# Chain transfers through DRAM issued from GpSimd's queue instead of SyncE's, in a two-layer hybrid trunk

## Chip, cores and metric

The kernel runs on one core of one Trainium2 chip. The metric is the device time of one execution, in microseconds; the time of a version is the median of its runs.

## What is computed

The reference is a causal trunk of two layers over 1024 tokens of 1024 channels, in float32. Each layer is a norm, a wide input projection, two token mixers side by side, an output projection and a gated MLP with a causal convolution of width 3. Layer 0 mixes with GLA (4 heads) and S5 (16 groups of 16 channels); layer 1 with RWKV-7 (8 heads of 64) and Mamba-2 (8 heads in 2 groups).

```python
for i in range(DEPTH):                       # two layers
    h = rms_norm(x, norm_mix[i])
    if i % 2 == 0:
        p = h @ e_w_in[j]
        ya = gla_mixer(p[..., :GLA_COLS], ...)
        yb = s5_mixer(p[..., GLA_COLS:], ...)
        x = x + jnp.concatenate([ya, yb], axis=-1) @ e_w_out[j]
    else:
        p = h @ o_w_in[j]
        yc = rwkv7_mixer(p[..., :RWKV_COLS], ...)
        yd = mamba2_mixer(p[..., RWKV_COLS:], ...)
        x = x + jnp.concatenate([yc, yd], axis=-1) @ o_w_out[j]
    h = rms_norm(x, norm_ffn[i])
    x = x + conv_glu_ffn(h, ffn_w_up[i], ..., ffn_w_down[i])
return rms_norm(x, norm_final)
```

Three places of the mixers matter here. GLA takes `b = jnp.cumsum(gc, axis=2)`, the running sum of its log decays. S5 gives `y = Re(C s) + d * u` and then `gelu(y)` and a gate. RWKV-7 divides keys by their length and its outputs by their standard deviation, head by head, and Mamba-2 normalizes its output group by group: a reciprocal root of one number for each token and head (or group).

## The kernel before

The 1024 tokens are done in two halves of 512 (`h` is 0 or 1). The projections are the bulk: each weight is split into a high and a low part and each product is three matmuls of 128x512 (`mm3`). `wunit` brings one unit of weights: SyncE loads 256 KB into `wr`, ScalarE rounds it to `wh`, VectorE takes the remainder `wl`. There are three buffers each of `wr`, `wh` and `wl`, so SyncE's next load waits until VectorE has read the buffer.

The mixers are generators that run beside the projections. `tick` advances them by the time that the projection's matmuls are thought to give; the scheduler that builds the program then places every instruction by a simulated time and a priority, so that the order on each engine is fixed when the program is built. On the chip each engine, and each engine's DMA issuing, goes through its own list in order: an instruction that waits holds back everything that stands behind it there. Buffers of the mixers come from small arenas (`k2`, `k4`, `kf`, and `mx` in PSUM).

In before nearly every DMA is issued by SyncE: weights, the projections' outputs to DRAM and back, and the mixers' own detours through DRAM. `self.MQ` and `self.Q` are both SyncE's queue; `self.AQ` is ScalarE's, which issues 14 small stores. The detours that the change touches:

- `rsqrt_rows` (14 times, in layer 1 alone: per half once for the keys, once for each of four RWKV pairs, once for each of two Mamba groups): one row per head lies in PSUM; ScalarE copies it to SBUF and issues a store (L463); a load brings it back spread over 128 partitions (`sm`, L467); VectorE does some 12 small operations; a store (L469) puts the roots into DRAM.
- `rows_to` (36 transfers): loads a row of roots broadcast over 64 or 128 partitions (L476). For the keys it fills `kk` in `rwkv_prep`; for outputs it fills `sq`, and VectorE multiplies by it next.
- GLA: `gla_decays` stores the four heads' running sums (L662), `gla_head` loads its own (L681), 8 of each.
- S5: the output `ys` (512 KB) goes to DRAM (L1045) and comes back in 8 loads of 32 KB for each of two tiles (`yf`, L1053), 32 loads in all. After each tile's eight loads VectorE forms `y`, ScalarE squares it, and so on to the gate.

GpSimd has little to do in before: it zeroes buffers (`tp` of S5 at L965, `Zs` of each RWKV pair at L1327) and clears a small tile `idle` 14 times for each `lagging` (L226); the latter only push the scheduler's placement of matmuls, and no matmul waits for them on the chip.

The tiles in the sections below: `acc` is a projection's PSUM, `kf` its copy in SBUF, `mh` and `ml` the split outputs of the mixers that the output projection reads, `yl` their load from DRAM, `dr` a buffer in DRAM, `k` any arena buffer.

Of the kernel before, what the change touches and what calls it, by code (L numbers as in the profile page):

```python
# [23 lines left out]
T = L // NH  # L24
# [104 lines left out]
class Kernel:  # L129
    def __init__(self, ctx, tc, a, dump=None):  # L130
        self.tc, self.nc, self.a = tc, tc.nc, a
        self.dump = dump
        nc = tc.nc
        self.V, self.A, self.G, self.PE, self.Q = nc.vector, nc.scalar, nc.gpsimd, nc.tensor, nc.sync
        self.MQ = nc.sync

        self.AQ = nc.scalar
        pool = lambda name, **kw: ctx.enter_context(tc.tile_pool(name=name, **kw))
        self.cp = pool("const", bufs=1)
        wp, mp = pool("stream", bufs=1), pool("mix", bufs=1)  # L140
        pp = pool("psum", bufs=1, space=PSUM)
        self.dp = pool("scratch", bufs=1, space=DRAM)
        self.uid = 0
        self.steps, self.ticks = None, 0
        self.rbc, self.rtok = [None] * NH, [None] * NH
        self.cost, self.ready, self.side = 0.0, set(), None
        self.wr = Ring(wp, "wr", WB[0], 512)
        self.wh = Ring(wp, "wh", WB[1], 512, F32R)
        self.wl = Ring(wp, "wl", WB[2], 512, F32R)
        self.xh = Ring(wp, "xh", KT, T, F32R)  # L150
        self.xl = Ring(wp, "xl", KT, T, F32R)
        self.mh = Ring(wp, "mh", MR, T, F32R)
        self.ml = Ring(wp, "ml", MR, T, F32R)
        self.yr = Ring(wp, "yr", YB[0], T)
        self.yl = Ring(wp, "yl", YB[1], T)
        self.rb = Ring(mp, "rb", 2, T)
        self.smr = Ring(mp, "sm", 24, 32)
        self.lsr = Ring(mp, "ls", 8, 32)
        self.smf = Ring(mp, "smf", 8, 8)
        self.zfr = Ring(mp, "zf", 2, 2 * RN)  # L160
        self.r0r = Ring(mp, "r0", 2, 2 * RN)
        self.gsr = Ring(mp, "gs", 2, GV)
        self.lsf = Ring(mp, "lsf", 2, 8)
        self.junk = mp.tile([128, GV], F32, name="junk")
        self.accr = Ring(pp, "acc", 4, 512)
        self.k2a, self.k4a, self.kfa = Arena(mp, "k2", K2, 520), Arena(mp, "k4", K4, 1024), Arena(mp, "kf", KF, 514)
        self.mxa = Arena(pp, "mx", 4, 512)
        self.wsa = Arena(mp, "ws", 2, 512)
# [288 lines left out]
    def rsqrt_rows(self, src, scale, bias, op1):  # L457

        p, n = src.shape[0], src.shape[0] * T // 128
        row = self.k2([p, T])  # L460
        self.act(row, src)
        d = self.dram([2, p, T])
        self.AQ.dma_start(d[0], row)  # L463
        self.fr(row)
        spread = lambda i: d[i].rearrange("a (q n) -> (a q) n", n=n)
        x = self.sm(n)
        self.MQ.dma_start(x, spread(0))  # L467
        self.ts(x, x, scale, bias, MUL, op1)
        self.MQ.dma_start(spread(1), self.rsqrt(x, n))  # L469
        return d[1]  # L470

    def rows_to(self, t, rows):

        w = 128 // rows.shape[0]
        for i in range(rows.shape[0]):
            self.MQ.dma_start(t[w * i:w * i + w], rows[i:i + 1].to_broadcast([w, T]))  # L476


    def norm_stats(self, h, t0=0, n=T, get=None, far=False):
# [158 lines left out]
    def gla_decays(self, h, wa2, alo):  # L638
# [17 lines left out]
        for hd in range(GH):  # L656
            n, b = N[hd // 2][:, hd % 2], self.k2()
            self.stt(n, E[hd // 2][:, hd % 2], -1.0, n, MUL, ADD)
            for c in range(NT):
                s = slice(c * 128, c * 128 + 128)  # L660
                self.V.tensor_tensor_scan(b[:, s], self.ones, n[:, s], 0.0, op0=MUL, op1=ADD)
            self.MQ.dma_start(self.st_b[h][hd], b)  # L662
            self.fr(b)
            yield
        self.fr(*E, *N)
# [3 lines left out]
    def gla_head(self, h, hd):  # L669
        yield from self.need(("gla", h, hd))  # L670
        qk, v, g, sg = self.k4([128, 2, T]), self.k4([128, NT, GV]), self.k4([128, NT, GV]), self.k4([128, NT, GV])
# [6 lines left out]
        self.fr(g)  # L678
        yield
        b = self.k2()  # L680
        self.MQ.dma_start(b, self.st_b[h][hd])  # L681
        c4 = lambda t: t.rearrange("p (c t) -> p c t", c=NT)
        cs = lambda c: slice(c * 128, c * 128 + 128)
        att = self.k2()
# [292 lines left out]
    def s5(self, h):  # L977
# [7 lines left out]
        for half in range(2):  # L985
            for ri in range(2):
                m = self.loaded(self.Ind[ri, half], [128, 512])
                for gg in range(8):
                    g = half * 8 + gg
# [7 lines left out]
        t = self.k2([128, 8, SN])  # L997
# [3 lines left out]
        for ri in range(2):  # L1001
# [7 lines left out]
            w = self.k2([128, 8, SN + 1])  # L1009
# [8 lines left out]
        t = self.k2([128, 8, SN + 1])  # L1018
# [6 lines left out]
        yd = self.dp.tile([SJ, SC, SG, SN], F32, tag="s5yd", bufs=2, name=self.nm("s5yd"))  # L1025
        ys = self.k4([128, SG, SN])
        ps = [self.mx([128, 8, SN]) for _ in range(2)]
        for half in range(2):
            ca = [self.loaded(self.CAd[ri, half], [128, 4, 128]) for ri in range(2)]
            tp = [self.loaded(self.Tpd[half, :, q * 4:q * 4 + 4], [128, 4, 128]) for q in range(2)]  # L1030
            for gg in range(8):
                g = half * 8 + gg
# [9 lines left out]
            self.act(ys.rearrange("p (a b) n -> p a b n", b=2)[:, :, i], ps[i])  # L1042
        self.fr(*ps)
        yield
        self.Q.dma_start(yd.rearrange("j c g n -> (j c) g n"), ys)  # L1045
        self.fr(ys, U, *X)
        yield
        z = []
        for tl in range(2):
            u = self.loaded(self.st_u[h][tl], [128, SJ, SN])  # L1050
            yf = self.k2([128, SJ, SN])
            for g in range(8):
                self.Q.dma_start(yf[16 * g:16 * g + 16], yd[:, :, tl * 8 + g, :].rearrange("j c n -> c j n"))  # L1053
            y = self.k2()
            yv = y.rearrange("p (c j) -> p j c", j=SJ)
            self.stt(yv, u, self.col("s5d", tl), yf, MUL, ADD)
# [847 lines left out]
```

## Time and profile before

| | |
|---|---|
| median of 3 runs | 2765.3 us (2763.23 to 2768.43) |
| the profiled execution | 2759.85 us |
| its span, first to last instruction | 2758.1 us |
| TensorE busy | 2663.3 us (97%) |
| VectorE busy | 1902.5 us (69%) |
| ScalarE busy | 1133.8 us (41%) |
| GpSimd busy | 79.1 us (3%) |
| mean granted TensorE clock | 0.980 |

A matmul's time is modelled and overlaps the next one's, so that 97% means that TensorE seldom lacked work, not that it worked at its peak; idle time in front of a matmul is what a wait costs. Waits are attributed to the instruction or DMA whose semaphore came last. DMA queue q1 is SyncE's and q10 ScalarE's; there is none of GpSimd's in the trace of before.

### The profile page before, as it was taken

Reading aid. Unit: us, or ns where it says so; the run is one execution under the profiler, and the core shown is the slowest. Engines: PE = TensorE matmul, PEld = TensorE weight load, DVE = VectorE, ACT = ScalarE, POOL = GpSimd, SP = SyncE. Lnnn points to the kernel's source line nnn. Section 1 sums busy time; section 2 is a strip of 40 time slices with the busy share of each in tenths; the row PEclk is TensorE's granted clock in tenths of the full one; section 3 lists DMA queues with packets and bytes.
Section 4 is the critical chain, followed back from the end, with each engine's and each line's share of the span. In section 5 each row is a group of like instructions: output and inputs, shape, how many; then the busy total and the mean of one; then the engine's idle time right before and its main releaser. Section 6 shows DMA issues by size and latency. Waiting matters only on the chain.

```text
span 2758.1 us, 39904 instructions
## 1 busy us (share of the span) xinstructions
PE 2663.3 (97%) x13804; PEld 2134.5 (77%) x13804; DVE 1902.5 (69%) x4538; ACT 1133.8 (41%) x2035; POOL 79.1 (3%) x462
## 2 busy tenths in 40 slices
PE   8999899999999999999999999999999998999998
PEld 6878788888888867777787777777687776788886
DVE  6987268766356665868586876768676687867557
ACT  4554255443234433433344544343333354434333
POOL 0000000000000000000220000000004000000000
PEclk9999799999899999999999999999999999999999
DMA  7555464434234554433343556443333345434333
GB/s 220 173 162 168 125 185 112 112 108 141 78 109 119 157 164 130 110 85 110 82 117 92 135 158 183 127 123 100 91 96 88 89 134 134 127 96 127 96 97 87
DMA packets 279602, 340.83 MB, mean 124 GB/s; under 512 B 101988, under 2 KB 137508, under 8 KB 279400
## 3 DMA queue, kind: packets, MB, share of 16 engines
q1 hardware_dynamic: 279168, 338.12, 43.2%
q8 instruction: 108, 1.77, 0.3%
q14 instruction: 94, 0.77, 0.1%
q10 hardware_dynamic: 232, 0.17, 0.0%
HBM read 286.91 MB, written 49.63 MB: 122 GB/s over the span
## 4 chain that ended last, share of the span: by engine, by line
PE 58%; DVE 7%; DMA 4%; issue 2%; ACT 1%; SPq 0%; POOL 0%; DVEq 0%; ACTq 0%
PE acc L340 49%; PE mx L340 8%; DMA k<-dr 3%; DVE k L215 2%; DVE k L245 1%; DVE wl L215 1%; DVE kf L245 1%; DMA yl<-dr 1%; ACT k L210 1%; ACT wh L210 0%; PE mx L347 0%; DVE x L215 0%; DMA dr<-kf 0%; DVE ml L215 0%; DMA rb<-dr 0%
## 5 line engine op out<-in xcount | busy, mean ns | idle before, releaser
L210 ACT ACTIVATE wh<-wr 128x512 fp32r<-128x512 f32 (+1 forms) x802 | 496.3, 620 | 933.0 <-PE acc L340 798.8
L215 DVE TENSOR_TENSOR wl<-wr,wh 128x512 fp32r<-128x512 f32 (+1 forms) x800 | 541.3, 678 | 417.9 <-ACT wh L210 378.9
L340 PE MATMUL acc<-xh,wh 128*128 128x512 f32 x2000 | 795.7, 399 | 16.8 <-ACT xh L210 9.6
L340 PE MATMUL acc<-xl,wh 128*128 128x512 f32 x2000 | 791.1, 396 | 0.1
L340 PE MATMUL acc<-xh,wl 128*128 128x512 f32 x1984 | 783.6, 396 | 7.1 <-DVE wl L215 7.0
L340 PEld LDWEIGHTS acc<-xh,wh 128*128 128x128 f32 x2000 | 377.3, 189 | 111.7 <-ACT xh L210 14.7
L340 PEld LDWEIGHTS acc<-xh,wl 128*128 128x128 f32 x1984 | 375.6, 189 | 89.6 <-DVE wl L215 10.0
L340 PEld LDWEIGHTS acc<-xl,wh 128*128 128x128 f32 x2000 | 377.1, 189 | 82.7 <-issue 3.8
L340 PE MATMUL acc<-mh,wh 128*128 128x512 f32 (+1 forms) x972 | 386.4, 399 | 25.4 <-DVE x L215 13.7
L340 PE MATMUL acc<-ml,wh 128*128 128x512 f32 (+1 forms) x972 | 385.5, 397 | 0.0
L340 PE MATMUL acc<-mh,wl 128*128 128x512 f32 (+1 forms) x972 | 383.3, 395 | 0.3 <-DVE wl L215 0.3
L215 DVE TENSOR_TENSOR k<-k,k 128x64 f32<-128x64 f32 (+27 forms) x894 | 284.6, 331 | 38.2 <-ACT k L210 19.2
L340 PEld LDWEIGHTS mx<-k,k 128*64 128x64 f32 (+5 forms) x2572 | 215.2, 154 | 82.1 <-issue 20.2
L340 PE MATMUL mx<-k,k 128*64 128x64 f32 (+9 forms) x2572 | 261.2, 256 | 11.0 <-DVE yr L215 3.5
L340 PEld LDWEIGHTS acc<-mh,wh 128*128 128x128 f32 x972 | 184.8, 190 | 68.4 <-issue 8.1
L340 PEld LDWEIGHTS acc<-mh,wl 128*128 128x128 f32 x972 | 184.1, 190 | 37.1 <-issue 2.1
L340 PEld LDWEIGHTS acc<-ml,wh 128*128 128x128 f32 x972 | 184.6, 190 | 34.0 <-issue 1.0
L210 ACT ACTIVATE k<-mx 128x512 f32<-128x512 f32 (+5 forms) x160 | 80.4, 512 | 176.6 <-PE mx L340 142.2
L210 ACT ACTIVATE k<-k 128x512 f32<-128x512 f32 (+4 forms) x176 | 109.0, 627 | 90.7 <-DVE k L215 46.2
L215 DVE TENSOR_TENSOR x<-acc,x 128x512 f32<-128x512 f32 (+1 forms) x196 | 123.2, 671 | 28.5 <-PE acc L340 28.1
L215 DVE TENSOR_TENSOR k<-k 128x256 f32<-128x256 f32 (+4 forms) x267 | 88.4, 357 | 26.0 <-DMA k<-dr 22.9
L245 DVE SCALAR_TENSOR_TENSOR kf<-acc,cols,kf 128x511 f32<-128x511 f32 (+1 forms) x132 | 98.3, 745 | 3.4 <-ACT kf L210 2.5
(178 smaller groups left out, 2360.8 us busy)
## 6 DMA issues: line engine op xcount, KB each, us to landing
wr<-wup SPq DMA_DIRECT2D x352, 256.0 KB
wr<-wdn SPq DMA_DIRECT2D x176, 256.0 KB
wr<-w1fm SPq DMA_DIRECT2D x104, 256.0 KB
dr<-kf SPq DMA_DIRECT2D x72, 256.0 KB
k<-dr SPq DMA_DIRECT2D x72, 256.0 KB
yl<-dr SPq DMA_DIRECT2D x64, 256.0 KB
wr<-wout SPq DMA_DIRECT2D x64, 256.0 KB
wr<-w0fm SPq DMA_DIRECT2D x40, 256.0 KB
```

Of the source, the lines that this page charges most:

```text
L210: self.made = self.A.activation(out, in_, f, **kw)
L215: self.made = self.V.tensor_tensor(out, a, b, op=op)
L245: self.made = self.V.scalar_tensor_tensor(out, a, s, b, op0=op0, op1=op1)
L340: return self.PE.matmul(out, lhsT, rhs, start=start, stop=stop)
```

## The change

A second name, `GQ`, is given to GpSimd's queue, and eight `dma_start` calls are moved to it: in a run 14 + 14 + 36 transfers of the roots, 8 + 8 of GLA's decays and 2 + 32 of S5's outputs, 114 in all. What they move, their buffers and the waits on their data stay. Line numbers grow by two.

```diff
         self.MQ = nc.sync
+
+        self.GQ = nc.gpsimd
 ...
-        self.MQ.dma_start(x, spread(0))
+        self.GQ.dma_start(x, spread(0))
         self.ts(x, x, scale, bias, MUL, op1)
-        self.MQ.dma_start(spread(1), self.rsqrt(x, n))
+        self.GQ.dma_start(spread(1), self.rsqrt(x, n))
 ...
         for i in range(rows.shape[0]):
-            self.MQ.dma_start(t[w * i:w * i + w], rows[i:i + 1].to_broadcast([w, T]))
+            self.GQ.dma_start(t[w * i:w * i + w], rows[i:i + 1].to_broadcast([w, T]))
 ...
-            self.MQ.dma_start(self.st_b[h][hd], b)
+            self.GQ.dma_start(self.st_b[h][hd], b)
 ...
-        self.MQ.dma_start(b, self.st_b[h][hd])
+        self.GQ.dma_start(b, self.st_b[h][hd])
 ...
-        self.Q.dma_start(yd.rearrange("j c g n -> (j c) g n"), ys)
+        self.GQ.dma_start(yd.rearrange("j c g n -> (j c) g n"), ys)
 ...
-                self.Q.dma_start(yf[16 * g:16 * g + 16], yd[:, :, tl * 8 + g, :].rearrange("j c n -> c j n"))
+                self.GQ.dma_start(yf[16 * g:16 * g + 16], yd[:, :, tl * 8 + g, :].rearrange("j c n -> c j n"))
```

Since the scheduler simulates the queues, the order on other engines moves too. Three places are shown.

SyncE's list in the first half of layer 0, where S5's outputs come back (`k20_165` is the second tile's `yf`, `wout0` the output projection's weights); before:

```order
L1053 DMA k20_165<-s5yd_111_2697 16x8x64
L417 DMA wr1_70<-wout0 128x512
L1053 DMA k20_165<-s5yd_111_2697 16x8x64 x2
L417 DMA wr2_71<-wout0 128x512
L1053 DMA k20_165<-s5yd_111_2697 16x8x64
L417 DMA wr0_69<-wout0 128x512
L1053 DMA k20_165<-s5yd_111_2697 16x8x64 x3
```

In the change the same loads stand on GpSimd's list, between GLA's decays of the two halves (`k26_171` is the first tile's `yf`):

```order
L683 DMA k29_174<-dr_58_283 128x512
L1047 DMA s5yd_111_2697<-k47_183 128x1024
L1055 DMA k26_171<-s5yd_111_2697 16x8x64 x8
L1055 DMA k20_165<-s5yd_111_2697 16x8x64 x8
L664 DMA dr_59_284<-k22_167 128x512
```

The store and the sixteen loads now follow each other with no load of weights between.

ScalarE's list at the same place. `k28_173` is the second tile's `y`, `k24_169` its square; `kf1` to `kf3` empty the PSUM banks `acc1` to `acc3`, which the output projection's first matmuls write next. Before:

```order
L210 ACTIVATE wh0_72<-wr0_69 128x512
L210 ACTIVATE k24_169<-k28_173 128x512
L210 ACTIVATE kf1_186<-acc1_162 128x384
L210 ACTIVATE kf2_187<-acc2_163 128x384
L210 ACTIVATE kf3_188<-acc3_164 128x384
L210 ACTIVATE k24_169<-k24_169 128x512
L210 ACTIVATE kf0_185<-acc0_161 128x512
```

In the change:

```order
L212 ACTIVATE kf1_186<-acc1_162 128x384
L212 ACTIVATE kf2_187<-acc2_163 128x384
L212 ACTIVATE wh1_73<-wr1_70 128x512
L212 ACTIVATE kf3_188<-acc3_164 128x384
L212 ACTIVATE wh2_74<-wr2_71 128x512
L212 ACTIVATE wh0_72<-wr0_69 128x512
L212 ACTIVATE kf0_185<-acc0_161 128x512
L212 ACTIVATE k24_169<-k28_173 128x512
```

The copies out of `acc` stood behind the square of the second tile; now they stand ahead of it.

GpSimd's list in layer 1, second half: the end of the last RWKV pair and the two Mamba groups, in the change (before, the list has at this place only the memsets, all in a row):

```order
L471 DMA dr_148_15773<-sm3_115 128x8
L478 DMA k21_166<-dr_148_15773 64x512 x2
L228 MEMSET idle_213 128x64 x84
L469 DMA sm9_121<-dr_149_16251 128x4
L228 MEMSET idle_213 128x64 x14
L471 DMA dr_149_16251<-sm10_122 128x4
L478 DMA k21_166<-dr_149_16251 128x512
L228 MEMSET idle_213 128x64 x84
L469 DMA sm13_125<-dr_150_16780 128x4
```

The chain's transfers and the memsets of `lagging` now take turns in one list.

## Rows read from the trace of the kernel before

**Rows 1.** The page: busy time, share of the span and instructions by engine.
```profile
PE 2663.3 (97%) x13804; PEld 2134.5 (77%) x13804; DVE 1902.5 (69%) x4538; ACT 1133.8 (41%) x2035; POOL 79.1 (3%) x462
```
**Rows 2.** TensorE's group by line: busy, mean ns | idle before, with releasers.
```profile
L340 PE MATMUL acc<-mh,wh 128*128 128x512 f32 (+1 forms) x972 | 386.4, 399 | 25.4 <-DVE x L215 13.7 <-ACT kf L210 7.3 <-ACT mh L210 2.4
```
**Rows 3.** Waits of SyncE's queue: us in total, times, longest.
```profile
SPq L417 <- DVE wl L215: 958.7, 478, 11.4
...
SPq L467 <- DMA dr<-k: 54.9, 10, 10.1
...
SPq L1045 <- ACT k L210: 30.9, 2, 17.4
```
**Rows 4.** Timeline of SyncE's queue: S5's outputs come back; a later spread load (start, us).
```profile
293.26 0.32 SPq L1045 DMA_DIRECT2D s5yd<-k  x1
...
299.87 0.37 SPq L1053 DMA_DIRECT2D k<-s5yd  x1
...
331.99 1.37 SPq L1053 DMA_DIRECT2D k<-s5yd  x3
...
1606.68 0.42 SPq L467 DMA_DIRECT2D sm<-dr  x1
```
**Rows 5.** Timelines of VectorE, ScalarE and TensorE just after [idle before <-releaser].
```profile
335.43 1.14 DVE L245 SCALAR_TENSOR_TENSOR k<-k,cols,k 128x512 f32<-128x512 f32 x1 [3.86 <-DMA dr<-kf]
...
336.60 0.63 ACT L210 ACTIVATE k<-k 128x512 f32<-128x512 f32 x1 [5.76 <-DVE k L245]
337.14 1.23 ACT L210 ACTIVATE kf<-acc 128x384 f32<-128x384 f32 x3
...
337.67 0.79 PE L340 MATMUL acc<-mh,wh 128*128 128x512 f32 x1 [7.27 <-ACT kf L210]
```
**Rows 6.** Busy time by stretch: PE, PEld, DVE, ACT, POOL, PEclk, DMA share, GB/s.
```profile
300.00:330.00 30.00, 30.00 (x152) 26.82 (x151) 10.77 (x18) 9.36 (x17) 0.00 (x0) 1.00 0.45 122
...
338.00:342.00 4.00, 4.00 (x8) 2.18 (x8) 1.54 (x3) 1.69 (x4) 0.00 (x0) 0.57 0.78 268
342.00:346.00 4.00, 4.00 (x18) 3.09 (x17) 3.38 (x6) 2.33 (x4) 0.00 (x0) 1.00 0.92 272
...
2300.00:2304.00 4.00, 3.98 (x13) 3.28 (x14) 3.36 (x11) 0.00 (x0) 0.00 (x0) 0.59 0.60 87
```
**Rows 7.** Timeline of TensorE: waits after which work on SyncE or VectorE came late.
```profile
1559.76 0.60 PE L340 MATMUL acc<-mh,wh 128*128 128x512 f32 x1 [1.86 <-DVE kf L245]
...
1869.78 0.50 PE L340 MATMUL acc<-xh,wl 128*128 128x512 f32 x1 [2.57 <-DVE wl L215]
...
1993.27 0.62 PE L340 MATMUL acc<-xh,wl 128*128 128x512 f32 x1 [2.74 <-DVE wl L215]
...
2300.02 0.47 PE L340 MATMUL acc<-mh,wh 128*128 128x512 f32 x1 [4.34 <-DVE x L215]
```
**Rows 8.** Pieces of the chain that ended last: start, us from issue to landing.
```profile
901.61 1.81 DMA dr<-smf
...
1548.83 3.42 DMA dr<-sm
...
1552.31 3.48 DMA k<-dr
```
**Rows 9.** Who waited for the loads of L476, then of L681: us, times.
```profile
  DVE k L215: 7.9, 7
  DVE k L245: 4.3, 2
  DVE yr L245: 4.0, 2
...
  DVE k L215: 7.7, 5
```
**Rows 10.** GpSimd: its memsets of 128x1024, by form; the longest run of small ones.
```profile
L1327 POOL MEMSET k<- 128x1024 f32 x8 | 7.6, 954 | 1880.6 <-DVE k L215 1789.6 <-PE mx L340 91.1
...
1359.09 41.38 POOL L226 MEMSET idle<- 128x64 f32 x196
```

## Prediction

> **What bounds the kernel now.** I read the busy times first: TensorE is busy 97% of the span, every other engine much less, GpSimd 3% [rows 1]. So SyncE's transfers cost time only where a matmul waits, and the question for each moved transfer is who behind it makes TensorE idle. The waits of SyncE's queue come next [rows 3]: 958.7 us are weight loads that wait for a buffer; they run ahead of need and are no loss in themselves. But 54.9 us are spread loads of `rsqrt_rows` that wait for their row's store, and 30.9 us are the two `ys` stores of S5, one of them 17.4 us long: while they wait, no weight behind them is fetched. Then the groups of matmuls by what ended their idle time: the output projections' group `acc<-mh,wh` idled 25.4 us, of which 7.3 in front of one copy `kf` of ScalarE and 13.7 behind VectorE [rows 2]. The timeline shows that copy's place: the matmul at 337.67 in layer 0's first half, with 7.27 us idle ahead of it, the longest wait of TensorE in the execution [rows 5].
>
> **S5's return, the gain.** The chain there reads backwards: the matmul at 337.67 waited for `kf` at 337.14; that stood in ScalarE's list behind the square at 336.60, which had ScalarE idle for 5.76 us until VectorE's `y` of 335.43 was there; VectorE had idled 3.86 us [rows 5] for the second tile's `yf`, whose last three loads were issued at 331.99 [rows 4]. The sixteen loads began at 299.87 and took 32 us because each shared SyncE's list with weight loads that wait for buffers: a circle, since a buffer comes free only through VectorE and TensorE. In the changed order store and loads stand together on GpSimd's list, and the copies `kf1` to `kf3` stand ahead of the square on ScalarE's, so two independent things break the chain. With p for one load's issue on GpSimd, and 2 us from the last issue to `y` (a bound: 335.43 less 331.99 and its 1.37, [rows 4, 5]), `y` is ready at 299.87 + 16p + 2. It has to be ready 7.27 us earlier than 335.43, at 328.2, so p may be 1.64 us. SyncE's own issue takes 0.32 to 0.42 [rows 4]; a GpSimd memset of 128x1024 takes 0.95 [rows 10], which gives 317. No GpSimd transfer is in this trace, so p is open; I take a value between these two, and the wait goes.
>
> With it goes a second loss. From 338 to 342 the granted clock was 0.57 (2.4 GHz is 1.00, 1.2 GHz half) after TensorE had idled 7.27 us, and 8 matmuls ran in 4 us where the next 4 us held 18 [rows 6]. By the clock that is 4 x 0.43 = 1.7 us lost, by the count 4 - 8 x 4/18 = 2.2; I take 1.9. S5: -7.3 - 1.9 = **-9.2 us**. Cover: what would come next is weights, and DMA engines were 0.45 busy from 300 to 330 [rows 6], so faster loads do not collide. In the second half the same loads have no wait of TensorE behind them; there I count nothing.
>
> **SyncE set free.** Two matmuls at 1869.78 and 1993.27 waited 2.57 and 2.74 us for VectorE's `wl` [rows 7], whose weights come through SyncE, behind spread loads that waited up to 10.1 us [rows 3]. Whether weights or VectorE's own list were late there the trace doesn't decide. Both ends: nothing, or 5.3 us with about 1.6 us of half clock behind each (4 x 0.41 where the clock was 0.59, [rows 6]), 8.5 in all. I take a third, **-2.8 us**, since VectorE is busy with the mixers at these places and the weights have three buffers of cover.
>
> **The chains, the cost.** One `rsqrt_rows` has three moved legs. The spread load is followed by VectorE work that has others' work ahead of it; I count it covered. Store and rows are on the chain: 28 legs, and 8 loads of GLA's decays, 36 in all. A leg on SyncE took from 1.81 us (an unloaded one) to 3.42 and 3.48 [rows 8]. On GpSimd the unknown is what issuing adds. Lower end: nothing is added, and a leg no longer stands behind weights, 1.81 in place of 3.42, a gain. Upper end: it adds a GpSimd operation of that size, 0.95 us [rows 10]. I take half of it, 0.475, nearer to the top than the middle of -1.61 and 0.95, because most rows were loaded as soon as the store had landed, so that little queueing is there to win back. 36 x 0.475 = 17.1 us of additional wait on VectorE. How much of that reaches TensorE? VectorE waited 7.9 + 4.3 + 4.0 us for the rows and 7.7 for the decays, 23.9 us [rows 9], and of TensorE's waits only 1.86 (1559.76) and 4.34 (2300.02) [rows 7] have a moved leg right behind them: 6.2 of 23.9, or 0.26. 17.1 x 0.26 = **+4.4 us**. It is spread in pieces of 0.1 us, so I add no half clock. Bounds: -9.5 (both waits vanish with the 1.6 of half clock behind each) and, with 0.95 and all of the wait counted up to 0.6, 36 x 0.95 x 0.6 = +20.5.
>
> By the Trainium skill, "DMA: Bandwidth & Descriptors", section Specifications, a transfer on the GpSimd path has its first byte after about 1 us, against 0.6 on the path of SyncE and ScalarE. No run here shows either; an estimate by its difference of 0.4 would make the chain term 36 x 0.4 x 0.26 = 3.7 instead of 4.4, and the sum 0.7 lower.
>
> **Memsets in GpSimd's way.** The small memsets of `lagging` now share the list: 196 take 41.38 us [rows 10], 0.21 each. 84 of them (17.7 us) stand between one Mamba group's rows, loaded from 1552.31 [rows 8], and the next group's spread load, which SyncE issued at 1606.68 [rows 4]: 54 us apart, covered. 14 (3 us) stand between spread load and store, where twelve small VectorE operations and a landing lie between: covered. The `Zs` memsets (8 of 0.95 [rows 10]) wait for a buffer that TensorE reads and stand behind the keys' rows; a late one would hold a pair's work and the row loads behind it, but their wait was for buffers and not for the queue. Nothing is added for these; if the cover is gone, a chain is late by a run's 3 to 18 us once.
>
> **Sum.** -9.2 - 2.8 + 4.4 = -7.6 us. The profiled execution took 2759.85, 5.45 below the median of the three runs, 2765.3; the difference is carried to the median: **2757.7 us**, 0.27% faster.
>
> **The rivals.** *No change.* The loads of S5 come earlier, but the output projection's first matmuls wait at the same place for something else: the weights, which stream at 268 to 272 GB/s with DMA engines 0.78 to 0.92 busy just behind the wait [rows 6], or VectorE, which was 10.77 of 30 us busy before it [rows 6] and so is not likely it. If the wait and its half clock return in full, the gain of 9.2 goes, and -2.8 + 4.4 remain: 2766.9; without the other two 2765.3. For it speaks that the circle holds for the weights too; against it that DMA engines were 0.45 busy for the 30 us ahead [rows 6]. The Trainium skill, "DMA: Bandwidth & Descriptors", section Rules for kernel authors, says that spreading transfers over several issuing engines doesn't help bandwidth, since all run on the same 16 engines, and "only saves sequencer issue time". By that rule this rival would hold; the row of 0.45 says bandwidth was not what was short in the 30 us ahead.
>
> *Slower.* GpSimd's legs are dear, and the engines' fixed order passes it on: in layer 1 VectorE is the engine on which `wl` and the chains meet, and each microsecond that its next instruction waits holds every `wl` behind it. With 0.95 us per leg and 0.6 of it reaching TensorE, +20.5 against the gain of 9.2: +11.3, or 2776.6. It decides from where the legs outweigh 9.2 + 2.8 = 12 us: 36 x 0.26 is 9.4, so from 1.3 us per leg at 0.26, or from 0.56 at 0.6. For it: the waits at 1559.76 and 2300.02, the second with a clock of 0.59 behind it [rows 6, 7]. Against it: TensorE takes 0.26 now, and weights of three buffers cover the rest.
>
> *The change doesn't do what it says:* GpSimd does not run ahead. If one load's issue takes 2.1 us or more, 299.87 + 2 + 16 x 2.1 = 335.5 is where `y` was before, and S5's wait stays but for the order of the copies: -2.8 + 4.4 = +1.6, 2766.9. The Trainium skill, "SBUF — State Buffer", section SBUF: two separate sides, says that descriptors of GpSimd's transfers are written by GpSimd through ports that certain VectorE operations lock, so that a transfer looks blocked while one runs. No run here shows it. VectorE was busy 10.77 of the 30 us [rows 6], so even if all of it locked GpSimd out, 19 us are left for sixteen issues, 1.2 us each.
>
> **How the numbers follow.** My forecast 0.53, no change 0.19, slower 0.22, GpSimd not running ahead 0.06. About 0.2% (5.5 us) is what a measurement can tell from no change: faster means below 2759.8, slower above 2770.8. The forecast lies 2.1 below that limit with an uncertainty of some 6 from the chains and the weights, so of its 0.53 I give 0.38 to faster and 0.15 to same. No change gives 0.04 to faster (a part of the wait goes), 0.14 to same and 0.01 to slower; the slower rival 0.22 to slower; the last 0.05 to same and 0.01 to slower. Faster 0.42, same 0.34, slower 0.24. Range: low end S5 and the whole of the two weight waits, -9.2 - 8.5, or 2747; high end the slower rival, 2776, with half of that case above it. Beyond both lies about 0.2.
>
> **What would show it.** In the changed profile: the wait `acc<-mh,wh` behind ScalarE's `kf` (7.3 us) and the clock of 0.57 behind it gone; SyncE's waits of 54.9 and 30.9 gone from its list and found on GpSimd's; sixteen loads on GpSimd's queue in under 26 us; VectorE's waits for rows and decays between 24 and 41 us. I am wrong if these grow past 60 us, if the largest wait of TensorE stands at the same place with another releaser, or if the layer-1 stretches show more half clock than before.

## The result: 0.63% slower

The changed kernel takes 2782.4 us (median of 5 runs, 2774.4 to 2791.6) against 2765.3 before (5 runs, 2760.0 to 2768.4). The ratio is 1.0063, interval 1.0045 to 1.0080: some 17 us slower. I had forecast 2757.7, in a range that ended at 2776.

The waits at S5's return, the largest that the prediction went after, are gone. In the changed profile (page: busy time by engine, then the group of the output projections; line numbers are two higher than before) TensorE's idle time of 7.3 us behind ScalarE's `kf` [rows 2] no longer stands there, and what VectorE's `x` ends has grown from 13.7 to 25.8 us:

```profile
PE 2669.7 (96%) x13804; PEld 2140.1 (77%) x13804; DVE 1899.6 (68%) x4538; ACT 1133.1 (41%) x2035; POOL 139.4 (5%) x576
...
L342 PE MATMUL acc<-mh,wh 128*128 128x512 f32 (+1 forms) x972 | 389.4, 402 | 25.8 <-DVE x L217 25.8
```

The two profiled executions are 22.2 us apart (spans 2758.1 and 2780.3). TensorE's busy time for the same 13804 matmuls grew by 6.4 of it, with a mean granted clock of 0.977 in place of 0.980; the other 15.8 us are idle time of TensorE.

The waits of SyncE's queue for S5's stores and the spread loads [rows 3] are gone from it too, and its weight loads wait longer (958.7 us before). The waits for the chains' data now stand on GpSimd (engine, line, releaser: us in total, times, longest):

```profile
SPq L419 <- DVE wl L217: 1049.2, 467, 18.6
...
POOL sm L469 <- DMA dr<-k: 909.6, 14, 264.2
...
POOL s5yd L1047 <- ACT k L212: 271.7, 2, 150.8
...
POOL dr L471 <- DVE sm L247: 118.6, 14, 12.3
```

S5's return looks as hoped. GpSimd's timeline (start, us of issuing, count) has the store at 306.74 and the sixteen loads in 10 us, where SyncE took 32 [rows 4], and the granted clock from 338 to 342 is 1.00 in place of 0.57 [rows 6] (windows: PE, PEld, DVE, ACT, POOL busy, PEclk, DMA share, GB/s):

```profile
306.74 0.54 POOL L1047 DMA_DIRECT2D s5yd<-k  x1 [120.91 <-ACT k L212]
310.32 5.77 POOL L1055 DMA_DIRECT2D k<-s5yd  x11 [3.04 <-DVE wl L217]
317.50 2.60 POOL L1055 DMA_DIRECT2D k<-s5yd  x5 [1.40 <-DMA k<-s5yd]
```
```profile
330.00:338.00 8.00, 7.95 (x37) 6.31 (x36) 3.98 (x8) 4.27 (x8) 0.00 (x0) 1.00 0.67 215
338.00:342.00 4.00, 4.00 (x19) 3.31 (x18) 1.82 (x2) 1.23 (x3) 0.00 (x0) 1.00 0.57 161
```

The cost of an issue on GpSimd also lies within the prediction's bracket. Groups of its transfers (busy, mean ns of one issue | idle before) show 0.53 to 0.57 us for an issue; the list of transfers (count, KB each, median us from issue to landing) gives what a leg then takes:

```profile
L478 POOL DMA_DIRECT2D k<-dr x36 | 18.8, 527 | 59.0 <-DVE k L217 16.9 <-issue 15.0 <-DMA dr<-sm 14.9
...
L469 POOL DMA_DIRECT2D sm<-dr x14 | 8.0, 572 | 909.6 <-DMA dr<-k 909.6
```
```profile
k<-dr POOLq DMA_DIRECT2D x12, 256.0 KB, 3.8
dr<-k POOLq DMA_DIRECT2D x8, 256.0 KB, 5.3
```

And VectorE's waits for the moved loads (who waited: us, times; L478, then L683) grew from 23.9 us [rows 9] to 39.7, by 15.8 where the sum had 17.1:

```profile
  DVE yr L247: 10.8, 4
  DVE k L217: 9.2, 6
  DVE k L247: 4.6, 2
```
```profile
  DVE k L217: 15.1, 5
```

So the two large pieces that the prediction priced, S5's return and the waits for the legs, came out about as priced, and the total has the other sign. What is missing shows when the traces are laid side by side at the same amount of work: the start of the matmul that writes `acc` with n such matmuls ahead of it, in us, and how much later than in before the other kernels reach it. Each column is one profiled execution, and they show where steps lie better than what they add up to: before's execution was 5.5 us below its median, and the one in before's order on GpSimd's queue, which ends 14.5 us behind, was 4.2 above its own, so that only about 4 us stand between the medians.

| n | before | the change | change's order, SyncE's queue | before's order, GpSimd's queue | S5 alone moved |
|---|---|---|---|---|---|
| 400 | 118.5 | +9.1 | +5.7 | +3.0 | +0.6 |
| 600 | 186.7 | +16.2 | +13.1 | +1.8 | -0.5 |
| 800 | 265.0 | +9.4 | +6.0 | +3.2 | +0.9 |
| 1000 | 345.0 | +0.0 | -2.5 | +0.3 | -7.0 |
| 1400 | 434.2 | +6.5 | +4.0 | +0.1 | -7.3 |
| 3000 | 880.3 | +2.5 | -1.0 | -2.2 | -9.4 |
| 5200 | 1521.4 | +2.2 | +2.2 | +6.9 | -7.4 |
| 5400 | 1583.8 | +14.4 | +12.6 | +7.6 | -7.7 |
| 7400 | 2171.3 | +15.7 | +13.9 | +11.9 | -4.8 |
| 8200 | 2413.5 | +22.5 | +16.1 | +14.5 | -2.2 |

In the change 16 us are lost before 187 us, in layer 0, before S5's return is reached. S5 gives back 9.4 between 800 and 1000 matmuls, near the 9.2 of the sum. Another 6.5 go between 345 and 434, 12 at the end of layer 1's first half, 7 more after 2171. The first of these places holds none of the roots, only GLA's decays.

### The profile page after: what moved, and what is told of

The parts are those of the page before. It is cut to its first block, busy times and chain, and to the rows that moved or that the text cites. A ratio compares the mean times of both kernels' runs of the same rounds, so it can differ in the third digit from the quotient of the medians.

```text
span 2780.3 us, 40023 instructions
## 1 busy us (share of the span) xinstructions
PE 2669.7 (96%) x13804; PEld 2140.1 (77%) x13804; DVE 1899.6 (68%) x4538; ACT 1133.1 (41%) x2035; POOL 139.4 (5%) x576
## 5 line engine op out<-in xcount | busy, mean ns | idle before, releaser
L342 PE MATMUL acc<-mh,wh 128*128 128x512 f32 (+1 forms) x972 | 389.4, 402 | 25.8 <-DVE x L217 25.8
L342 PE MATMUL mx<-k,k 128*64 128x64 f32 (+10 forms) x2572 | 260.3, 255 | 12.0 <-DVE yr L217 6.2
L342 PEld LDWEIGHTS acc<-mh,wh 128*128 128x128 f32 x972 | 185.6, 191 | 67.9 <-issue 15.7
```

The source lines that it names most:

```text
L342: return self.PE.matmul(out, lhsT, rhs, start=start, stop=stop)
```

## Experiments

**How order and queue were taken apart.** The change does two things: it moves transfers to another queue, and it makes the scheduler place instructions of TensorE, VectorE and ScalarE in another order, since it simulates that queue. To have one without the other, a kernel is built twice in one file. The first build uses one choice of queue and only its order is kept; the second uses the other choice, and an ordering edge without a wait ties each instruction to the one ahead of it on its engine:

```diff
-        self.GQ = nc.gpsimd
+        self.GQ = getattr(nc, QUEUE)
...
     with tile.TileContext(nc) as tc:
         build(tc, aps)
+        block = nc.cur_bb.bb
+        made = {i.name: i for i in block.instructions if not type(i).__name__.startswith("BassTile")}
+        last = {}
+        for name in order:
+            i = made.get(name)
+            if i is not None:
+                if i.engine in last:
+                    tc.add_manual_dep(i, last[i.engine], none, reason="order")
+                last[i.engine] = name
...
+    nc, _ = program(ins, "gpsimd", program(ins, "sync")[1])
```

All lists of the three engines are then those of the first build, instruction by instruction; on SyncE and GpSimd, too, each transfer keeps its place relative to the others of its queue. In the traces the three lists of a pinned run agree by kind of operation and tile with those of the run whose order it has, at all but two of VectorE's 4538 places. Between before and the change VectorE's lists differ at 1747 places, and at 1197 when the roots alone are moved, 506 for GLA and 64 for S5. Pinning by itself costs nothing that shows (GLA in before's order: 1.0002). Theory O is that the order costs, theory L that the legs on GpSimd's queue cost. Ratios are against the kernel before on the same chip.

| transfers on GpSimd | order of the engines made for | ratio | interval |
|---|---|---|---|
| all 114 (the change) | all on GpSimd | 1.0063 | 1.0045 to 1.0080 |
| none | all on GpSimd | 1.0028 | 1.0015 to 1.0041 |
| all | none (before's order) | 1.0016 | 1.0002 to 1.0029 |
| all | S5 on GpSimd | 1.0013 | 0.9998 to 1.0029 |
| S5 | S5 on GpSimd | 0.9975 | 0.9962 to 0.9987 |
| none | S5 on GpSimd | 0.9969 | 0.9955 to 0.9982 |
| GLA | GLA on GpSimd | 1.0057 | 1.0042 to 1.0072 |
| none | GLA on GpSimd | 1.0035 | 1.0022 to 1.0048 |
| GLA | none (before's order) | 1.0002 | 0.9990 to 1.0013 |
| GLA's loads | GLA on GpSimd | 1.0061 | 1.0044 to 1.0078 |
| roots | roots on GpSimd | 1.0044, again 1.0057 | 1.0026 to 1.0062, 1.0041 to 1.0073 |
| none | roots on GpSimd | 1.0010 | 0.9999 to 1.0020 |
| roots | none (before's order) | 1.0014 | 1.0002 to 1.0026 |
| roots' spread loads and stores | roots on GpSimd | 1.0040 | 1.0028 to 1.0052 |
| roots' rows | roots on GpSimd | 1.0041 | 1.0028 to 1.0054 |
| GLA | GLA on GpSimd, one edge added | 1.0012 | 1.0002 to 1.0023 |

**All transfers, before's order.**

> All 114 transfers go through GpSimd's queue as in the change, but TensorE, VectorE, ScalarE and the rest of SyncE's list stand in exactly the order of the kernel before (the order is taken from a first build in which the transfers are SyncE's, and pinned in the second). Theory O (the order that the scheduler made from its view of the queues is what costs): the gain of S5 stays and the legs cost little, about -9 + 3, 2754 to 2763. Theory L (the legs on GpSimd's queue are what costs): as slow as the change, 2775 to 2785.

Measured: 1.0016, +4 us. The queue by itself costs a quarter of what the change costs, and theory L falls as the whole story. But S5's gain is not in it. GpSimd issues the loads in 9 us, the last at 308.50, and TensorE still waits 5.33 of its 7.27 us (GpSimd's timeline, then TensorE's):

```profile
300.16 7.86 POOL L1055 DMA_DIRECT2D k<-s5yd  x15 [3.25 <-PE acc L342]
308.50 0.53 POOL L1055 DMA_DIRECT2D k<-s5yd  x1 [0.48 <-DMA k<-s5yd]
```
```profile
337.39 0.80 PE L342 MATMUL acc<-mh,wh 128*128 128x512 f32 x1 [5.33 <-ACT kf L212]
```

The loads no longer hold anything there, but the order still does. VectorE's `y` comes at 333.14, without a wait of its own, behind a split of weights that had waited; ScalarE's square follows, and the first copy of `acc` behind it waits 1.92 us more for a store of `kf` (VectorE's timeline, then ScalarE's):

```profile
332.53 0.69 DVE L217 TENSOR_TENSOR wl<-wr,wh 128x512 fp32r<-128x512 f32 x1 [1.98 <-ACT wh L212]
333.14 1.13 DVE L247 SCALAR_TENSOR_TENSOR k<-k,cols,k 128x512 f32<-128x512 f32 x1
```
```profile
336.85 0.49 ACT L212 ACTIVATE kf<-acc 128x384 f32<-128x384 f32 x1 [1.92 <-DMA dr<-kf]
```

**No transfer moved, the change's order.**

> The reverse: the order of the changed kernel on TensorE, VectorE and ScalarE, but all 114 transfers are issued by SyncE. Theory O: as slow as the change or slower, 2775 to 2790, since the early places of consumers stay and S5's loads wait among weights again. Theory L: near or below the kernel before, 2755 to 2768.

Measured: 1.0028, +7.7 us, with every transfer back on SyncE: nearly half of the change's loss is the order alone. Its trace loses 13.1 us by 600 matmuls and 10.4 between 5200 and 5400, where the change loses 16.2 and 12.2. And it has S5's gain, 8.5 us between 800 and 1000, although S5's loads stand among weights again, the last of them issued at 335.51 (331.99 in before [rows 4], but this run is 6 us behind at 800 matmuls). VectorE still waits 1.09 us for that load. TensorE does not: its first matmul of the output projection starts at 338.86, ahead of ScalarE's square of the second tile at 339.85, so the copies of `acc` can't have stood behind that square. The timelines of SyncE, VectorE, ScalarE and TensorE, the last with its longest wait from 290 to 345:

```profile
335.51 0.43 SPq L1055 DMA_DIRECT2D k<-s5yd  x1
```
```profile
338.57 1.22 DVE L247 SCALAR_TENSOR_TENSOR k<-k,cols,k 128x512 f32<-128x512 f32 x1 [1.09 <-DMA k<-s5yd]
```
```profile
339.85 0.62 ACT L212 ACTIVATE k<-k 128x512 f32<-128x512 f32 x1
```
```profile
323.81 0.44 PE L342 MATMUL acc<-wh,xh 128*128 128x384 f32 x1 [0.69 <-ACT wh L212]
...
338.86 0.39 PE L342 MATMUL acc<-mh,wh 128*128 128x512 f32 x1
```

**S5 alone.** The other calls go back to SyncE:

```diff
-        self.GQ.dma_start(x, spread(0))
+        self.MQ.dma_start(x, spread(0))
...
-            self.GQ.dma_start(self.st_b[h][hd], b)
+            self.MQ.dma_start(self.st_b[h][hd], b)
```

> Only S5's 2 stores and 32 loads are moved; the scheduler orders the rest, which it leaves as before outside S5's return. Both theories: TensorE's wait of 7.3 us at 330 and the half clock behind it go, -9.2, so about 2756 (2753 to 2760). If instead the wait turns up at the same place for another reason, 2762 to 2767.

Measured: 0.9975, -7 us (2758.1 beside 2766.3). Then the same order with S5's loads on SyncE:

> The order that the scheduler makes when S5's transfers are GpSimd's, pinned on TensorE, VectorE and ScalarE, but S5's loads are issued by SyncE (at the places of that order in its list). If the gain of 8 us of moving S5 alone lies in the order (ScalarE's copies of acc ahead of the square), 2756 to 2761. If it lies in GpSimd's queue, 2763 to 2769.

Measured: 0.9969, -8.5 us, the fastest of all kernels here. The gain is real, near the size in the sum, and it is the order's; the queue has no measurable part in it. Which piece of the order gives it, this run alone does not show: beside ScalarE's copies ahead of the square, the loads have earlier places in SyncE's list too, the last of them at 322.97:

```profile
322.97 0.43 SPq L1055 DMA_DIRECT2D k<-s5yd  x1
```

The run with the change's order, above, has the loads late and the wait gone all the same. That speaks for the copies; they were not moved by themselves.

**The roots alone.**

> Only the transfers of the reciprocal roots are moved (layer 1). In the change layer 1 lost some 17 us between 1500 and 2390. Theory O and theory L both put that on this part: 2775 to 2785, with the layer 0 of the kernel before. If layer 1's loss came from the state that the earlier parts leave (their order), about 2765.

Measured: 1.0044; a second measurement:

> Only the roots moved, as in the earlier run (+12.2, interval 7 to 17), once more beside the others, since its order alone cost 2.8 and its queue alone 3.9. If the two simply add, +5 to +8; if they make each other worse, +10 to +15.

Measured: 1.0057. So the roots cost 12 to 16 us. Their order without the queue, and their queue without the order:

> The order of the kernel that moves only the roots, pinned, but the roots' transfers are issued by SyncE. Theory O: most of that kernel's +12 stays, 2772 to 2780, with the wait of 8.4 us at the end of layer 1's first half. Theory L: 2762 to 2769.

> The order of the kernel before, pinned, but the roots' transfers are issued from GpSimd's queue: the cost of the 64 legs by themselves. My sum's share for them, 28 legs at 0.12 us, was +3.5: 2768 to 2771. Theory O: that or less, 2765 to 2771. Theory L: the whole +12 of the roots, 2775 to 2781.

Measured: 1.0010 and 1.0014, 2.8 and 3.9 us (the first is not clear of no change), together about half of what both at once cost. The queue's 3.9 is near my share of 3.5. The order's own mark stands where expected, at the end of layer 1's first half. TensorE's wait behind VectorE there, in the change, in the order of the roots with all transfers on SyncE, and in before's order with all on GpSimd:

```profile
1584.72 0.77 PE L342 MATMUL acc<-mh,wh 128*128 128x512 f32 x1 [8.30 <-DVE x L217]
```
```profile
1574.79 0.77 PE L342 MATMUL acc<-mh,wh 128*128 128x512 f32 x1 [7.97 <-DVE x L217]
```
```profile
1567.54 0.79 PE L342 MATMUL acc<-mh,wh 128*128 128x512 f32 x1 [2.78 <-DVE kf L247]
```

The 8 us wait follows the order and not the queue; behind it the change's clock falls to half speed for some 6 us (windows of the change, PEclk is the third number from the right):

```profile
1584.00:1588.00 4.00, 3.28 (x10) 2.65 (x11) 3.99 (x12) 3.40 (x9) 0.00 (x0) 0.50 0.06 18
1588.00:1592.00 4.00, 4.00 (x17) 2.87 (x16) 3.29 (x8) 0.56 (x2) 0.00 (x0) 0.67 0.00 0
```

Part of it had been gained just before: between 5000 and 5200 matmuls the change wins back 5.4 us on before, and the roots' order on SyncE's queue 4.4, ahead of the 12.2 and 10.0 that they lose by 5400. I read this as projections that run ahead of the mixers and a TensorE that waits when that work is used up; no run tests it.

**GLA alone.**

> Only GLA's 16 transfers of decays are moved, with the order that the scheduler then makes. If the parts add (change +17, S5 -7, roots +12), +12: 2774 to 2782, lost before 440 us. If they don't, and S5's gain in the change makes up what GLA's order loses ahead of it, near 2766.

Measured: 1.0057, 15.7 us for sixteen transfers, the dearest part of the change. Order and queue apart:

> The order that the scheduler makes when GLA's 16 transfers of decays are GpSimd's, pinned on TensorE, VectorE and ScalarE, but the transfers are issued by SyncE. Moving them with that order cost 0.57%, 15.7 us. If the order costs (theory O), +9 to +14, with the same losses between 60 and 190 us and between 390 and 435. If the queue does (theory L), within 3 us of before.

> The order of the kernel before, pinned, and GLA's 16 transfers issued from GpSimd's queue. Theory O: +0 to +4 and no loss between 60 and 190 us. Theory L: +12 or more.

Measured: 1.0035 and 1.0002. The queue alone is free; the order alone costs 9.7 us; both cost 6 more than that, which is no more than the two intervals allow for. The first place shows a part of it. VectorE's list of the change, from its 326th row on (`k20` holds the loaded decays; `k22`, `k26` and `k29` are small steps of S5; the same steps filled rows 327 to 340 before, with the first operation on `k20` in row 344, behind the splits `wl2` and `wl0`):

```
326 L247 SCALAR_TENSOR_TENSOR kf4_189<-acc2_163,rb0_110 128x512
327 L217 TENSOR_TENSOR k26_171<-k26_171,k22_167 128x4x16
328 L217 TENSOR_TENSOR k25_170<-k20_165 128x256
```

VectorE goes through its list in order. In the change it reaches that operation at 108 and waits 3.35 us for the decays, with 13 steps of S5 behind it that could run. TensorE's next matmuls are now GLA's products of these decays, `mx<-k`, and wait 6.84 us (VectorE's timeline, then TensorE's, of the change):

```profile
111.42 0.90 DVE L217 TENSOR_TENSOR k<-k 128x256 f32<-128x256 f32 x3 [3.35 <-DMA k<-dr]
```
```profile
114.34 1.94 PE L342 MATMUL mx<-k 128*128 128x64 f32 x8 [6.84 <-DVE k L217]
```

Before, the small steps lay ahead of the decays and covered the transfer. TensorE's next matmuls were S5's, which waited 3.20; GLA's came 7 us later and did not wait:

```profile
109.94 1.97 PE L347 MATMUL mx<-cons,k 128*128 128x128 f32 x8 [3.20 <-DVE k L215]
...
116.65 1.08 PE L340 MATMUL mx<-k 128*128 128x64 f32 x8
```

With GLA's order and SyncE's queue VectorE does not wait at all there (108.19), since the load could be issued 3.5 us behind its store and not 5.7 as on GpSimd. GpSimd's timeline of the change, SyncE's and VectorE's of that run:

```profile
101.50 0.68 POOL L664 DMA_DIRECT2D dr<-k  x1 [99.81 <-ACT wh L212]
...
107.24 0.55 POOL L683 DMA_DIRECT2D k<-dr  x1 [3.63 <-DMA dr<-k]
```
```profile
101.12 0.32 SPq L664 DMA_DIRECT2D dr<-k  x1
...
104.65 0.53 SPq L683 DMA_DIRECT2D k<-dr  x1
```
```profile
108.19 0.89 DVE L217 TENSOR_TENSOR k<-k 128x256 f32<-128x256 f32 x3
```

So here order and queue need each other: the order takes the cover away, and the longer leg then shows.

The order costs something at this place without any such wait, too. With it on SyncE's queue TensorE waits 3.41 and 1.29 us, hardly more than the 3.20 and 1.10 of before, and yet that run is 6.6 us behind at 400 matmuls. About half of this is clock: behind its waits TensorE first goes on with small products of the mixers where before had the projection, and the granted clock is back at 0.98 from 116 on in before, but 0.50 until 124 in that run. Summed over the six stretches of 4 us from 104 to 128, the clock takes 3.4 us more there (windows of before, then of that run):

```profile
116.00:120.00 4.00, 4.00 (x28) 3.70 (x27) 3.75 (x11) 1.13 (x2) 0.00 (x0) 0.98 0.92 287
120.00:124.00 4.00, 4.00 (x29) 3.85 (x28) 3.60 (x13) 1.68 (x3) 0.00 (x0) 1.00 0.95 270
```
```profile
116.00:120.00 4.00, 3.41 (x16) 3.04 (x17) 2.91 (x6) 1.72 (x4) 0.00 (x0) 0.50 0.20 76
120.00:124.00 4.00, 4.00 (x15) 4.00 (x15) 3.01 (x10) 0.00 (x0) 0.00 (x0) 0.50 0.66 205
```

A second place of GLA's is the order's alone: at 405.16 in the change TensorE waits 4.27 us for `kf`, and 5.21 in GLA's order with SyncE's queue; in before the matmul at that place waited 0.17. It is S5's place the other way round. In the change's list of ScalarE the copies of `acc` stand behind an operation of the mixers that waits 5.05 us for a load `k<-dr`; in before they stood ahead of it (ScalarE's timeline of the change, then TensorE's of the change, of GLA's order on SyncE, and of before):

```profile
401.55 1.28 ACT L212 ACT_TABLE_LOAD   x1 [5.05 <-DMA k<-dr]
```
```profile
405.16 0.50 PE L342 MATMUL acc<-xh,wh 128*128 128x512 f32 x1 [4.27 <-ACT kf L212]
```
```profile
408.97 0.80 PE L342 MATMUL acc<-xh,wh 128*128 128x512 f32 x1 [5.21 <-ACT kf L212]
```
```profile
398.04 0.50 PE L340 MATMUL acc<-xh,wh 128*128 128x512 f32 x1 [0.17 <-ACT kf L210]
```

**One edge added to GLA's order.** `I-1181` is the first operation on the decays, `I-1564` the split `wl0`:

```diff
+EDGES = [('I-1181', 'I-1564')]
...
+        for late, early in EDGES:
+            tc.add_manual_dep(made[late], early, none, reason="order")
```

> Only GLA's transfers moved, the scheduler's own order, but with one edge: VectorE's first operation on the loaded decays of head 0 may not stand ahead of the split of the weights that it stood behind before. If the first loss of that kernel (9.6 us by the 400th projection matmul, TensorE's wait of 7.3 us at 107) comes from this one place, the wait shrinks to the 3.4 us of before and the time is 6 to 10 us below that kernel's +15.7, at +5 to +10. If the loss comes from elsewhere in the order, +13 to +16.

Measured: 1.0012, 12 us faster than GLA alone without the edge, yet not in the way that was expected. TensorE's wait at this place stayed, 7.38 us, and 11.5 us were lost by 600 matmuls:

```profile
114.60 1.94 PE L342 MATMUL mx<-k 128*128 128x64 f32 x8 [7.38 <-DVE k L217]
```

VectorE waited 3.41 us there as well, now at another operation on the decays than the one that the edge had moved. Some of the time came back later: with 1200 matmuls done its trace is 1.0 us behind before, where GLA alone without the edge is 9.9. With the one edge the scheduler had made another order of the rest, with VectorE's list different at 325 places. As a proof of the place it failed; as a measure of how much hangs on the order, one edge moved 12 us.

**GLA's store or its load.**

> The order of the kernel that moves GLA alone, pinned; the 8 stores of decays by SyncE, the 8 loads from GpSimd's queue. That order took +9.7 with both on SyncE and +15.7 with both on GpSimd. If GpSimd's slower store (5.3 us to its landing, the load behind it 5.9 us after it, against 3.5 on SyncE) makes the difference, +9 to +11 and VectorE's wait of 3.6 us at 111 gone. If the load does, +14 to +16.

Measured: 1.0061. The first half of the expectation held at the place itself: with the stores on SyncE VectorE no longer waits there, and TensorE waits 3.41 us in place of 7.12 in the run of GLA alone:

```profile
109.71 1.94 PE L342 MATMUL mx<-k 128*128 128x64 f32 x8 [3.41 <-DVE k L217]
```

But the time did not follow. So the wait at 107 is explained, and the 6 us between order alone and both are not.

**The roots' legs.**

> The order of the kernel that moves the roots alone, pinned; the spread loads and the stores of roots (28) from GpSimd's queue, the broadcast rows (36) by SyncE. That order took +2.8 with all on SyncE and +12 to +16 with all on GpSimd. If the rows' loads make the difference, +3 to +6; if the spread loads and stores do, +9 to +14.

> The reverse: the 36 broadcast rows from GpSimd's queue, the 28 spread loads and stores by SyncE, in the same order. If the rows' loads make the difference, +9 to +14; if the others do, +3 to +6; if both have a share, both runs lie between, at +6 to +9.

Measured: 1.0040 and 1.0041, 11 us each. Neither leg is the culprit; either half on GpSimd costs nearly what both cost. Between the starts of a chain's transfers the traces of this order differ little: from spread load to store 9.27 us in the mean of 14 chains with all on SyncE, 9.77 with spread loads and stores on GpSimd; from store to first row 2.57 and 2.97 where the rows were GpSimd's. These are half a microsecond per chain, and the loss is spread over layer 1 in steps of 2 to 4 us.

**All transfers on GpSimd, S5's order.**

> All 114 transfers issued from GpSimd's queue, exactly as in the change, but TensorE, VectorE and ScalarE in the order that the scheduler makes when S5 alone is moved. Theory O (the change is slow for the order, and GpSimd's queue costs about 4): S5's order gives -8.5, the queue costs 0.5 (GLA) + 3.9 (roots): -4, faster than before. Theory L: +3 or more.

Measured: 1.0013. It was to be 4 us faster than before and is not measurably different; the same queue in the order of the change is 1.0063. So the order decides between these two by 0.5%, but GpSimd's queue costs 12 us in this good order (0.9969 to 1.0013), not the 4 that it costs in before's.

## Why the prediction was wrong

**What bounds the kernel** was read rightly: idle time of TensorE is most of what separates the two kernels, 15.8 of 22.2 us, and the rest goes with a lower granted clock. The wait at 337 was the largest but for the 8.0 us ahead of the very first matmul.

**S5's return** was -9.2; alone it measures -7 (interval 3.6 to 10.5), with the loads on SyncE -8.5. The size was right. The reason was half wrong. I had written that two independent things break the chain, the queue and the place of the copies. The loads on GpSimd in before's order left 5.33 of 7.27 us; the order with the loads on SyncE removed all of it, in the change's order with a load still late. The row behind VectorE's 3.86 us names a store, `dr<-kf` [rows 5]; I read it as the loads', and rightly so, since with early loads that wait is gone. But it was not the link to cut: what stood behind `y` and its square in ScalarE's list was.

**SyncE set free** was -2.8 and came to nothing. The two waits [rows 7] stand in the changed profile at nearly the size of before (2.57 and 2.74). TensorE's timeline at the first, then ScalarE's:

```profile
1886.00 0.50 PE L342 MATMUL acc<-xh,wl 128*128 128x512 f32 x1 [2.92 <-DVE wl L217]
```
```profile
1882.03 0.63 ACT L212 ACTIVATE wh<-wr 128x512 fp32r<-128x512 f32 x1 [1.47 <-issue]
```

VectorE's own list was late there and not the weights: for the wait that ends at 1886.00 ScalarE had begun the two `wh` at 1879.26 and 1882.03, and VectorE, without idle time in the 8 us ahead, came to their `wl` only at 1885.27 and 1886.29. At 2007.72 the wait is 2.47 us, and VectorE is again busy without a gap. SyncE's own waits are now for buffers.

**The chains** were +4.4. Issuing takes 0.53 us instead of 0.32 to 0.48, and the waits on VectorE grew by 15.8 where the sum had 17.1. In before's order the queue alone costs 4.4 (interval 0.5 to 8.0) for all transfers, 0.5 and 3.9 for GLA and the roots by themselves; there VectorE's waits for the moved loads are 36.4 us in the trace, 12.5 more than before, and 4.4 of 12.5 is 0.35 where I had 0.26. The step fits before's order. In the others the queue costs more: 12 in S5's order, 9.7 in the change's (1.0063 against 1.0028), though of these only the first is clear of 4.4 by the intervals, and just. The pass-through of 0.26 was taken from the cover that before's order gives, and the cover is part of the order.

**The memsets** cost nothing that shows, as said: all 14 spread loads and all 14 stores of the roots waited on GpSimd for their data and not for memsets. The rival by which GpSimd does not run ahead fell: one load's issue took 0.53 us, and 2.1 were needed. **The DMA engines** did not limit S5's return; the rival of no change fell. The Trainium skill's rule that it drew on ("DMA: Bandwidth & Descriptors", Rules for kernel authors: another issuing engine saves only sequencer time) agrees with the S5 runs all the same: with the order held, the other queue gained nothing there (0.9969 and 0.9975).

**The step that failed** is the order. I had seen that the change moves instructions, priced its effect at S5's return, and taken the rest at nothing without a reason. The prediction's signs of being wrong had the same gap: the waits for rows and decays stayed at 39.7 us, under the 60 named, and S5's place kept no wait, while the loss lay elsewhere. The order alone measures +7.7 with S5's -8.5 in it, so some +16 elsewhere: +9.7 for GLA, +2.8 for the roots, and some 4 that neither has alone, which is within the intervals. For GLA the sum had only eight loads at 0.475 x 0.26, about 1 us; moved alone, GLA costs 15.7, no less than the roots' 12 to 16. The comparison of the two orders showed VectorE's first operation on the decays sixteen rows earlier, ahead of the splits of weights; that was to be read, place by place, with the wait of the trace beside it. Of the order's cost two places are shown, at 107 and at 405 in layer 0, and one at the end of layer 1's first half; for the rest the runs give the sum and not the places.

**The rival** named slower had 2776.6, near the result, by legs that pass 0.6 of 0.95 us to TensorE. That nearness is luck: the same legs in before's order cost a quarter of the loss. Its condition, a VectorE that goes through its list in order and passes a wait on to what stands behind, is what the place at 107 shows, though there mixers' steps stood behind the wait and not `wl`.

**Open** is whether, and why, order and queue together cost more than one and the other: 15.7 against 10.2 for GLA, 12 to 16 against 6.7 for the roots, 17.4 against 12.1 for all. By the intervals of the table (an estimate) these excesses of some 5, 7 and 5 us are uncertain by about 6 each way, so that only the roots' is just clear of noise, and the pieces were not all measured on one chip; but all three point the same way. At one place an excess is shown (cover gone, leg longer). The runs with half of the legs back on SyncE did not bring the loss back in halves. And runs of one kernel scatter by 0.3% and more, the longer ones at a lower mean granted clock: of the change's five, the one of 2774.4 us had 0.978 and the one of 2791.6 had 0.973.

## What to carry to other kernels

Where a scheduler places instructions by simulated queues, moving a transfer to another queue is two changes, and the second can be the larger: build once with either queue, pin the order of one to the queues of the other, and measure all four. Price a change of order by the operations that now stand behind a wait on an in-order engine, at every place where the lists differ and not only at those that the change is for. A gain found by following a wait back through a transfer may be had from any link of the chain; here the order gave all of it with no transfer moved, by the traces through ScalarE's list. And read the granted clock beside the waits: at GLA's first place the order added hardly any wait and 3.4 us of half clock.

## What the runs showed of the hardware

An issue on GpSimd's queue took 0.53 to 0.57 us in the mean of a line, whatever it moved (2 KB to 512 KB), against 0.32 to 0.48 in the median for the same lines on SyncE. Most legs were not dear beside the 1.81 to 3.48 us of SyncE's [rows 8]: from issue to landing 2.0 us in the median for a store of roots (2 to 16 KB) to 3.8 for a load of 256 KB; but the store of GLA's decays, 256 KB, took 5.3 us in the median, and at GLA's first place the load behind it was issued 5.7 us after it where SyncE's came 3.5 after.

TensorE's clock fell behind the long waits: after the 8.30 us at 1584 it was granted 0.50 of full speed (1.2 GHz) for 4 us and 0.67 for the next 4. That wait cost some 3 us more than itself, (1 - 0.50) x 4 + (1 - 0.67) x 4 = 3.3. How long the clock stayed down was not set by the wait alone: after 3.20 and 1.10 us of waiting near 110 in before it was back at 0.98 from 116 on, with 28 matmuls in that stretch of 4 us; after 3.41 and 1.29 us in GLA's order it stood at 0.50 to 124, with 16 and 15 matmuls in the two stretches.
